# Mixed projection of a streaming encoder layer: where in the instruction stream the stationary operands of the next group are prepared

## The chip, the core and the metric

The kernel runs on one NeuronCore of a Trainium2 chip. The metric is the device time of one execution, in microseconds (us); a kernel's time is the median over its runs. Engines are called as in the profile: PE is TensorE (PEld its weight loads), DVE is VectorE, ACT is ScalarE, POOL is GpSimd, SP is SyncE. POOL and SP also issue DMAs, each in the order of its own queue.

## What is computed

One layer of a hybrid encoder for two groups of requests together: 256 new frames of one stream and 16 frames each of 8 running streams, 384 rows in all, model width 2048. The part that matters here is the second branch of the mixer and its gate:

```python
a_ssd = gated_rmsnorm(y.reshape(b, L, D_INNER), z, p['ssd_norm'])   # 384 rows x 4096
br_pool = a_pool @ p['w_pool_proj']
br_ssd = a_ssd @ p['w_ssd_proj']                                    # 4096 x 2048
merged = gates[:, :, 0] * br_pool + gates[:, :, 1] * br_ssd
out = merged @ p['w_out']
```

Everything is float32. Each product of two float32 matrices is made of three products of rounded parts: an operand is split into a high part (rounded copy, made by ACT) and a low part (the difference, made by DVE), and PE adds high x high, high x low and low x high.

## The kernel before, in words

The layer runs in stages: normed input projections, pooling branch, state-space branch, then the **mixed projection** (`a_ssd @ w_ssd` woven together with the gate projections), then `w_out` and the MLP. In all of them PE multiplies tiles of 128 partitions, and a weight tile of 128 x 1024 is brought in by SP, split by ACT (the `wh_` tile) and by DVE (the `wl_` tile), and used by PE.

In the mixed projection, the 4096 rows of `w_ssd` are cut into eight **groups** `gk` = 0 to 7, and a group's output columns into two **halves** of 1024 (`np_` = 0, 1). A 2 x 2 block product is done with seven multiplications instead of eight, so that a half consists of seven **forms**, in this order: `b11, b21, U, b22, W, V, X` (`ORDER`). A form is one weight tile: a block as loaded (`b11, b21, b22`) or a sum of blocks (`U, W, V, X`, built in place by POOL's adding DMA, L1136, and by DVE, L1159). So a group has fourteen forms, numbered here t = 0 to 13, and the stage has 112. A form multiplies its weight with one or two **slots**, stationary tiles that hold blocks of `a_ssd` or differences of them; there are ten slots to a group:

```python
USES = {"b11": ((0, 0), (7, 2)), "b21": ((1, 3), (7, 5)), "b22": ((2, 8), (8, 9)),
        "X": ((3, 4),), "U": ((4, 6),), "W": ((5, 7),), "V": ((6, 1), (8, 2))}   # form: (product, slot)
DIFFS = ((6, 1, 4), (7, 0, 6), (8, 3, 7), (9, 5, 2), (1, 1, 0))                 # slot o = slot a - slot b
KEYS = {"b11": (0,), "s2": (2,), "b21": (3, 5), "U": (6,), "b22": (8, 9), "W": (7,), "V": (1,), "X": (4,)}
```

For each group the slots are prepared in three steps while the group before is multiplied. `aload` (L1232) brings the six raw blocks into the tile `ax` with four DMAs on POOL's queue, at t = 4 of the group before. There is one `ax` tile, so these DMAs wait until the last reader of the old contents, the refill of `X` (DVE's `alX`), is done. `diffs` (L1241) makes the five differences with five subtractions of 128 x 256 on DVE. `refill` (L1248 and L1249) splits one or two slots: ACT writes the high part (`ahb`, `ahU`, `ahs` and so on), DVE the low part (`alb`, `alU`, `als`). The high and low tiles exist once for each key, twice for `s2`; a key is refilled after its last use in the old group and before its first in the new one.

`quad` gives for each form the steps `ready` (split the weight, L1123 on ACT and L1124 on DVE, and build the next sum on DVE, L1159) and `run` (its matmuls, L1172 to L1174, then the products that are complete are taken to `acs`, L1149 and L1151), and at the end of `run` calls `extra(t)`, which emits the step of preparation for that t. `later()` places such a step behind the weight splits that were emitted last on ACT and DVE.

Between the forms stand the gate projections `ga` and `gb` (L102 to L104, with splits at L71 and L72): after each half of a gate projection three or four forms follow. A finished gate is scaled on DVE (`gat`, L1330), put through a sigmoid on ACT and multiplied on DVE (L1334). Within these rules a scheduler sets the order of the instructions on each engine; each engine then works through its own list in that order.

Of the kernel before, what the change touches and what calls it, by code (L numbers as in the profile page):

```python
# [33 lines left out]
def build(ctx, tc, io):  # L34
# [18 lines left out]
    def sstile(name):  # L53
        return pss.tile([P, 512], F32, tag="ss", name=name)
# [23 lines left out]
    @contextmanager  # L78
    def later():
        with behind(cut[0]), behind(cut[1]):  # L80
            yield
# [294 lines left out]
    with tc.tile_pool(name="phc", bufs=1, reuse_waits="tile") as pc, tc.tile_pool(name="phc2", bufs=2, reuse_waits="tile") as pc2:  # L376
# [3 lines left out]
        for i in range(2):  # L380
            b = pc.tile([P, 640], F32, name=f"pbuf{i}")[:, :519]
# [210 lines left out]
    with tc.tile_pool(name="phd", bufs=2, reuse_waits="tile") as pd, tc.tile_pool(  # L592
# [5 lines left out]
        for i in range(3):  # L598
            b = pd1.tile([P, 24, 19], F32, name=f"cbuf{i}")
# [513 lines left out]
    DIFFS = ((6, 1, 4), (7, 0, 6), (8, 3, 7), (9, 5, 2), (1, 1, 0))  # L1113
# [121 lines left out]
        raw.append(x)  # L1235
        return i

    def diffs(gk):
        x = raw[gk]
        for o, a, b in DIFFS:  # L1240
            v.tensor_tensor(x[:, o], x[:, a], x[:, b], ALU.subtract)  # L1241

    def refill(gk, key):
        ss = KEYS[key]
        n = len(ss)
        src = raw[gk][:, ss[0] : ss[-1] + 1 : max(1, ss[-1] - ss[0])]
        h, l = (pqf.tile([P, n, 2, P], F32R, tag=f"a{a}{key}", name=f"a{a}{key}{gk}", bufs=2 if key == "s2" else 1) for a in "hl")
        s.activation(h, src, AF.Copy)  # L1248
        v.tensor_tensor(l, src, h.bitcast(F32), ALU.subtract)  # L1249
        for i, j in enumerate(ss):  # L1250
            slots[gk][j] = (h[:, i], l[:, i])

    def sp_quad(gk, np_):
        def part(slot, k2):
            h, l = slots[gk][slot]
            return h[:, k2], l[:, k2]

        def extra(i):
            t = np_ * 7 + i
            if gk and t < 3:  # L1260
                with later():
                    refill(gk, ("W", "V", "X")[t])
            if gk == 7:
                if t == 4:
                    early = pq.tile([P, 10, 2, P], F32, tag="ax", name="axe").rearrange("p s k t -> p (s k t)")
                    for n in range(3):
                        place[n] = early[:, n * 768 : n * 768 + 768]
                        fetch(n)
                elif t == 6:
                    todo.extend(converted(lambda m: acc[:, m]))  # L1270
                elif t > 6:
                    todo.pop(0)()
                return
            if t == 4:
                aload(gk + 1)
            with later():
                if t == 9:
                    diffs(gk + 1)
                elif t == 10:
                    refill(gk + 1, "b11")  # L1280
                    refill(gk + 1, "s2")
                elif t > 10:
                    refill(gk + 1, ("b21", "U", "b22")[t - 11])

        return quad(f"sq{gk}_{np_}", pqw, acc, np_, gk == 0, lambda i, nb: io["w_ssd"][nb, gk * 2 + i], part, extra)

    todo, place = [], {}

    def fetch(n):
        if n not in place:  # L1290
            place[n] = pqw.tile([P, 1024], F32, tag="wd", name=f"mw{n}", bufs=7)
        gp.dma_start(place[n][:, :T], gb_scr[n])
        gp.dma_start(place[n][:, T : 2 * T], ma_scr[n])
# [152 lines left out]
    with tc.tile_pool(name="phf", bufs=1, side="right", reuse_waits="tile") as pf, tc.tile_pool(  # L1446
# [80 lines left out]
        for nb in range(4):  # L1527
# [3 lines left out]
            o = [sstile(f"wo{nb}_{b}") for b in range(3)] if nb else o_first  # L1531
# [168 lines left out]
    with tc.tile_pool(name="phg", bufs=1, side="right", reuse_waits="tile") as pg, tc.tile_pool(  # L1700
# [83 lines left out]
        for nb in range(4):  # L1784
            o = [sstile(f"wd{c8}_{nb}_{b}") for b in range(3)]
# [161 lines left out]
```

## Time and profile before

| what | value |
|---|---|
| median of 3 runs | 2588.47 us (2587.6 to 2589.66) |
| profiled execution, its own time | 2588.24 us |
| its span (first to last instruction) | 2586.5 us |
| PE busy over the span | 2572.9 us (99%) |
| DVE, ACT, POOL busy over the span | 1951.8, 1599.2, 446.4 us |
| mixed projection, 1106 to 1452 us of the span | 346 us; PE busy 342.42, DVE 287.01, ACT 274.04 us |
| granted TensorE clock | 0.999 |

The profiled execution's own time is 1.7 us longer than its span. It lies 0.2 us under the median. Times in the rows are microseconds from the span's start. A row of the timeline has start, duration, engine, line, operation, and the tiles written and read, without their numbers; the brackets at its end say how long the engine stood before it, and what released it. The ends of matmuls are modelled: the profiler gives a 128 x 384 matmul 0.33 us though the next one starts 0.16 us after it. DVE and ACT rows may overlap in the same way, by about 0.1 us.

### The profile page before, as it was taken

How to read it: one execution, taken by the hardware profiler on the slowest of the kernel's cores; microseconds unless marked ns; L12 is line 12 of the kernel's file. 1: busy time of each engine (PE TensorE's matmuls, PEld its weight loads, DVE VectorE, ACT ScalarE, POOL GpSimd, SP SyncE). 2: the span in 40 equal slices, each digit the busy share in tenths (PEclk: the TensorE clock that was granted, in tenths of full speed). 3: DMA queues.
4: the chain of work that ended last, by engine and by line, in shares of the span. 5: the costliest groups of instructions: out<-in, count | busy, mean ns of one | idle time of the engine just before them, and what ended most of it. 6: DMA issues, size and time to landing. Idle time of an engine off the chain costs nothing.

```text
span 2586.5 us, 41046 instructions
## 1 busy us (share of the span) xinstructions
PE 2572.9 (99%) x15589; PEld 2448.1 (95%) x15589; DVE 1951.8 (75%) x2763; ACT 1599.2 (62%) x2520; POOL 446.4 (17%) x647
## 2 busy tenths in 40 slices
PE   9999999999999999999999999999999999999998
PEld 9999999999999999998888988999999999999997
DVE  6676367999999999678878855767777777777766
ACT  6443355657565665578878634666766667676653
POOL 0000043355444444111111200000000000000000
PEclk9999999999999999999999999999999999999999
DMA  7444566666766676676666555654555555455444
GB/s 280 150 134 160 166 224 211 226 217 229 240 223 223 222 242 223 213 247 186 205 200 188 179 205 193 205 161 148 156 161 165 168 157 153 150 161 163 139 139 171
DMA packets 141782, 490.43 MB, mean 190 GB/s; under 512 B 21728, under 2 KB 26144, under 8 KB 135824
## 3 DMA queue, kind: packets, MB, share of 16 engines
q1 hardware_dynamic: 100544, 355.93, 41.1%
q0 software_dynamic: 33984, 117.06, 15.7%
q10 hardware_dynamic: 7056, 14.81, 1.8%
q8 instruction: 122, 2.00, 0.3%
q14 instruction: 76, 0.62, 0.1%
HBM read 437.85 MB, written 49.87 MB: 189 GB/s over the span
## 4 chain that ended last, share of the span: by engine, by line
PE 96%; DVE 2%; ACT 1%; issue 1%; DMA 1%; DVEq 0%; POOL 0%; ACTq 0%; POOLq 0%
PE pj_up L102 6%; PE pj_up L104 6%; PE pj_up L103 6%; PE wd L1173 5%; PE wd L1174 5%; PE wd L1172 5%; PE pj_x L102 5%; PE pj_x L103 5%; PE pj_x L104 5%; PE pj_z L104 3%; PE pj_z L102 3%; PE pj_z L103 3%; PE sq L1173 2%; PE sq L1174 2%; PE sq L1172 2%; PE pj_pp L102 2%
## 5 line engine op out<-in xcount | busy, mean ns | idle before, releaser
L102 PE MATMUL pj_up<-x1h,wh_up 128*128 128x384 f32 (+1 forms) x1024 | 333.7, 326 | 0.0
L103 PE MATMUL pj_up<-x1l,wh_up 128*128 128x384 f32 (+1 forms) x1024 | 333.4, 326 | 0.0
L104 PE MATMUL pj_up<-x1h,wl_up 128*128 128x384 f32 (+1 forms) x1024 | 333.4, 326 | 0.0
L71 ACT ACTIVATE wh_up<-w_up 128x1024 fp32r<-128x1024 f32 x126 | 133.2, 1057 | 219.2 <-PE pj_up L103 206.1
L102 PE MATMUL pj_x<-xgh,wh_x 128*128 128x384 f32 x768 | 251.9, 328 | 0.0
L103 PE MATMUL pj_x<-xgl,wh_x 128*128 128x384 f32 x768 | 250.4, 326 | 0.0
L104 PE MATMUL pj_x<-xgh,wl_x 128*128 128x384 f32 x768 | 250.4, 326 | 0.0
L72 DVE TENSOR_TENSOR wl_up<-w_up,wh_up 128x1024 fp32r<-128x1024 f32 x126 | 154.1, 1223 | 56.3 <-ACT wh_up L71 56.2
L103 PEld LDWEIGHTS pj_up<-x1l,wh_up 128*128 128x128 f32 x1024 | 193.6, 189 | 2.6
L102 PEld LDWEIGHTS pj_up<-x1h,wh_up 128*128 128x128 f32 x1024 | 193.6, 189 | 2.6
L104 PEld LDWEIGHTS pj_up<-x1h,wl_up 128*128 128x128 f32 x1024 | 193.6, 189 | 0.0
L102 PE MATMUL pj_z<-xgh,wh_z 128*128 128x384 f32 x512 | 166.9, 326 | 0.0
L103 PE MATMUL pj_z<-xgl,wh_z 128*128 128x384 f32 x512 | 166.9, 326 | 0.0
L104 PE MATMUL pj_z<-xgh,wl_z 128*128 128x384 f32 x512 | 166.9, 326 | 0.0
L1136 POOL DMA_DIRECT2D w_b_wd<-w_down x28 | 24.2, 864 | 773.4 <-DMA w_b_wd<-w_down 682.9
L102 PEld LDWEIGHTS pj_x<-xgh,wh_x 128*128 128x128 f32 x768 | 145.1, 189 | 2.1 <-issue 0.4
L103 PEld LDWEIGHTS pj_x<-xgl,wh_x 128*128 128x128 f32 x768 | 145.2, 189 | 0.0
L104 PEld LDWEIGHTS pj_x<-xgh,wl_x 128*128 128x128 f32 x768 | 145.2, 189 | 0.0
L72 DVE TENSOR_TENSOR wl_x<-w_x,wh_x 128x1024 fp32r<-128x1024 f32 x96 | 116.7, 1220 | 29.2 <-ACT wh_x L71 29.2
L71 ACT ACTIVATE wh_x<-w_x 128x1024 fp32r<-128x1024 f32 x96 | 100.4, 1052 | 61.1 <-PE pj_z L103 30.5
L1149 ACT COPY acc<-wd 128x512 f32<-128x512 f32 x200 | 116.6, 583 | 22.8 <-PE wd L1174 22.7
L1172 PE MATMUL wd<-wh_b_wd,fh 128*128 128x512 f32 x336 | 127.3, 379 | 0.0
(478 smaller groups left out, 7832.3 us busy)
## 6 DMA issues: line engine op xcount, KB each, us to landing
w_up<-w_up SPq DMA_DIRECT2D x128, 512.0 KB, 4.0
w_b_wd<-w_down SPq DMA_DIRECT2D x112, 512.0 KB, 4.5
w_x<-w_in SPq DMA_DIRECT2D x96, 512.0 KB, 3.9
w_z<-w_in SPq DMA_DIRECT2D x64, 512.0 KB, 4.3
w_b_sq<-w_ssd SPq DMA_DIRECT2D x64, 512.0 KB, 4.7
w_ga<-w_ga SPq DMA_DIRECT2D x32, 512.0 KB, 4.6
w_pp<-w_pp SPq DMA_DIRECT2D x32, 512.0 KB, 3.5
hs<-ssm POOLq DMA_DIRECT2D x16, 1024.0 KB, 7.2
```

What stands on the lines that cost most here:

```text
L71: cut[0] = s.activation(h, w, AF.Copy)
L72: cut[1] = v.tensor_tensor(l, w, h.bitcast(F32), ALU.subtract)
L102: te.matmul(out, wh, xh, start=first, stop=False, **how)
L103: te.matmul(out, wh, xl, start=False, stop=False, **how)
L104: return te.matmul(out, wl, xh, start=False, stop=last, **how)
L1136: gp.dma_start(w, unit(0, np_ * 2), accum_op=ALU.add)
L1149: s.copy(dst, o)
L1172: te.matmul(out, mh, vh, start=begin, stop=False, skip_group_check=held)
L1173: te.matmul(out, mh, vl, start=False, stop=False, skip_group_check=held)
L1174: te.matmul(out, ml, vh, start=False, stop=end, skip_group_check=held)
```

## The change

The same operations are done on the same data; where they are emitted differs. Before, group gk + 1 was prepared in eight forms: t = 9 to 13 of group gk (`diffs`; `b11` and `s2`; `b21`; `U`; `b22`) and t = 0 to 2 of group gk + 1 (`W`, `V`, `X`). After, it is prepared in t = 6 to 13 and 0 to 3: `s2` at t = 6, three differences at t = 7 and two at t = 8, nothing at t = 9 and 10, `b11`, `b21`, `U` at t = 11, 12, 13, then `b22`, `W`, `V`, `X` at t = 0 to 3 of the new group. `diffs` takes a slice of the table for this. The load stays at t = 4. Lines behind the change have numbers smaller by one in the changed kernel (L1330 becomes L1329).

```diff
-    def diffs(gk):
+    def diffs(gk, which=slice(0, 5)):
         x = raw[gk]
-        for o, a, b in DIFFS:
+        for o, a, b in DIFFS[which]:
             v.tensor_tensor(x[:, o], x[:, a], x[:, b], ALU.subtract)
...
-            if gk and t < 3:
+            if gk and t < 4:
                 with later():
-                    refill(gk, ("W", "V", "X")[t])
+                    refill(gk, ("b22", "W", "V", "X")[t])
...
             with later():
-                if t == 9:
-                    diffs(gk + 1)
-                elif t == 10:
-                    refill(gk + 1, "b11")
+                if t == 6:
                     refill(gk + 1, "s2")
+                elif t in (7, 8):
+                    diffs(gk + 1, slice(0, 3) if t == 7 else slice(3, 5))
                 elif t > 10:
-                    refill(gk + 1, ("b21", "U", "b22")[t - 11])
+                    refill(gk + 1, ("b11", "b21", "U")[t - 11])
```

The pieces of the engines' lists below are from group 4. The names carry the group: `ax5` is the raw tile of group 5, `wl_W_sq4_1` the low weight part of form W in half 1 of group 4, `alb115` the low stationary part for `b11` of group 5; `alX4` belongs to group 4.

**Second half of group 4.** DVE before, from behind the split of `U` and the first of the five differences, to the gate's split:

```order
L1151 TENSOR_TENSOR acs_12341<-sq4_1_7_14424,acs_12341 128x512
L1159 TENSOR_TENSOR w_b12_sq4_1_14432<-w_b12_sq4_1_14432,w_b22_sq4_1_14439 128x1024
L1241 TENSOR_TENSOR ax5_14355<-ax5_14355 128x256 x4
L1124 TENSOR_TENSOR wl_b22_sq4_1_14531<-w_b22_sq4_1_14439,wh_b22_sq4_1_14530 128x1024
L1159 TENSOR_TENSOR w_b11_sq4_1_14435<-w_b12_sq4_1_14432,w_b11_sq4_1_14435 128x1024
L1249 TENSOR_TENSOR alb115_14551<-ax5_14355,ahb115_14550 128x256
L1249 TENSOR_TENSOR als25_14555<-ax5_14355,ahs25_14554 128x256
L1124 TENSOR_TENSOR wl_W_sq4_1_14559<-w_b12_sq4_1_14432,wh_W_sq4_1_14558 128x1024
L1159 TENSOR_TENSOR w_b21_sq4_1_14437<-w_b21_sq4_1_14437,w_b12_sq4_1_14432 128x1024
L1249 TENSOR_TENSOR alb215_14573<-ax5_14355,ahb215_14572 128x512
L1330 TENSOR_TENSOR gat12_14576<-pj_ga12_14363,rstd_197 128x384
L72 TENSOR_TENSOR wl_ga13_0_14583<-w_ga13_0_14580,wh_ga13_0_14582 128x1024
```

DVE after, from the same split of `U` on:

```order
L1159 TENSOR_TENSOR w_b12_sq4_1_14436<-w_b12_sq4_1_14436,w_b22_sq4_1_14443 128x1024
L1151 TENSOR_TENSOR acs_12341<-sq4_1_7_14424,acs_12341 128x512
L1124 TENSOR_TENSOR wl_b22_sq4_1_14535<-w_b22_sq4_1_14443,wh_b22_sq4_1_14534 128x1024
L1159 TENSOR_TENSOR w_b11_sq4_1_14439<-w_b12_sq4_1_14436,w_b11_sq4_1_14439 128x1024
L1159 TENSOR_TENSOR w_b21_sq4_1_14441<-w_b21_sq4_1_14441,w_b12_sq4_1_14436 128x1024
L1124 TENSOR_TENSOR wl_W_sq4_1_14555<-w_b12_sq4_1_14436,wh_W_sq4_1_14554 128x1024
L1249 TENSOR_TENSOR alb115_14569<-ax5_14355,ahb115_14568 128x256
L1329 TENSOR_TENSOR gat12_14572<-pj_ga12_14363,rstd_197 128x384
L72 TENSOR_TENSOR wl_ga13_0_14579<-w_ga13_0_14576,wh_ga13_0_14578 128x1024
L1333 TENSOR_TENSOR gat12_14572<-gat12_14572,ppt12_14396 128x384
L1124 TENSOR_TENSOR wl_V_sq4_1_14611<-w_b11_sq4_1_14439,wh_V_sq4_1_14610 128x1024
L1249 TENSOR_TENSOR alb215_14631<-ax5_14355,ahb215_14630 128x512
```

Four of the differences shown (the fifth stands one row ahead), `als25` and `alb215` no longer stand between the split of `U` and the split `wl_ga13_0`; `alb215` stands behind the split of `V`.

PE before, at the place where that gate projection begins:

```order
L1174 MATMUL sq4_1_5_14535<-wh_W_sq4_1_14558,alW4_14245 128x512
L102 MATMUL pj_ga13_14579<-xgh0_263,wh_ga13_0_14582 128x384
L103 MATMUL pj_ga13_14579<-xgl0_264,wh_ga13_0_14582 128x384
L1172 MATMUL sq4_1_6_14563<-wh_V_sq4_1_14614,ahV4_14298 128x512
L1172 MATMUL sq4_1_8_14517<-wh_V_sq4_1_14614,ahs24_14114 128x512
L104 MATMUL pj_ga13_14579<-xgh0_263,wl_ga13_0_14583 128x384
```

PE after, the same place:

```order
L1174 MATMUL sq4_1_5_14539<-wh_W_sq4_1_14554,alW4_14295 128x512
L102 MATMUL pj_ga13_14575<-xgh0_263,wh_ga13_0_14578 128x384
L103 MATMUL pj_ga13_14575<-xgl0_264,wh_ga13_0_14578 128x384
L104 MATMUL pj_ga13_14575<-xgh0_263,wl_ga13_0_14579 128x384
L102 MATMUL pj_ga13_14575<-xgh1_284,wh_ga13_0_14578 128x384
L103 MATMUL pj_ga13_14575<-xgl1_285,wh_ga13_0_14578 128x384
```

The two matmuls of form V that stood ahead of the first one with `wl_ga13_0` are gone from there; form V now follows the whole half projection.

**First half of group 4, the last reader of `ax4`.** DVE before, from the split of `U`:

```order
L1124 TENSOR_TENSOR wl_U_sq4_0_14303<-w_b12_sq4_0_14216,wh_U_sq4_0_14302 128x1024
L1249 TENSOR_TENSOR alX4_14318<-ax4_13953,ahX4_14317 128x256
L1159 TENSOR_TENSOR w_b12_sq4_0_14216<-w_b12_sq4_0_14216,w_b22_sq4_0_14223 128x1024
L1159 TENSOR_TENSOR w_b11_sq4_0_14219<-w_b12_sq4_0_14216,w_b11_sq4_0_14219 128x1024
L1159 TENSOR_TENSOR w_b21_sq4_0_14221<-w_b21_sq4_0_14221,w_b12_sq4_0_14216 128x1024
L1124 TENSOR_TENSOR wl_b22_sq4_0_14322<-w_b22_sq4_0_14223,wh_b22_sq4_0_14321 128x1024
L1151 TENSOR_TENSOR acs_12341<-sq4_0_7_14204,acs_12341 128x512
L1124 TENSOR_TENSOR wl_W_sq4_0_14342<-w_b12_sq4_0_14216,wh_W_sq4_0_14341 128x1024
```

DVE after, from the split of `U`:

```order
L1124 TENSOR_TENSOR wl_U_sq4_0_14299<-w_b12_sq4_0_14212,wh_U_sq4_0_14298 128x1024
L1249 TENSOR_TENSOR alV4_14314<-ax4_13953,ahV4_14313 128x256
L1159 TENSOR_TENSOR w_b12_sq4_0_14212<-w_b12_sq4_0_14212,w_b22_sq4_0_14219 128x1024
L1159 TENSOR_TENSOR w_b11_sq4_0_14215<-w_b12_sq4_0_14212,w_b11_sq4_0_14215 128x1024
L1159 TENSOR_TENSOR w_b21_sq4_0_14217<-w_b21_sq4_0_14217,w_b12_sq4_0_14212 128x1024
L1124 TENSOR_TENSOR wl_b22_sq4_0_14318<-w_b22_sq4_0_14219,wh_b22_sq4_0_14317 128x1024
L1151 TENSOR_TENSOR acs_12341<-sq4_0_7_14200,acs_12341 128x512
L1249 TENSOR_TENSOR alX4_14338<-ax4_13953,ahX4_14337 128x256
```

`alX4`, on which the four DMAs into `ax5` wait, stood right behind the split of `U` and now stands behind three sums, the split of `b22` and an addition to `acs`.

**End of the first half of group 4, the first reader of `ax5`.** ACT before, from the split of form X:

```order
L1123 ACTIVATE wh_X_sq4_0_14418<-w_b21_sq4_0_14221 128x1024
L1144 COPY sq4_1_0_14422<-acs_12341 128x512
L1144 COPY sq4_1_1_14445<-acs_12341 128x512
L1123 ACTIVATE wh_b11_sq4_1_14441<-w_b11_sq4_1_14435 128x1024
L1149 COPY acs_12341<-sq4_0_6_14346 128x512
L1123 ACTIVATE wh_b21_sq4_1_14460<-w_b21_sq4_1_14437 128x1024
```

ACT after:

```order
L1123 ACTIVATE wh_X_sq4_0_14418<-w_b21_sq4_0_14217 128x1024
L1144 COPY sq4_1_0_14422<-acs_12341 128x512
L1248 ACTIVATE ahs25_14432<-ax5_14355 128x256
L1144 COPY sq4_1_1_14449<-acs_12341 128x512
L1123 ACTIVATE wh_b11_sq4_1_14445<-w_b11_sq4_1_14439 128x1024
L1149 COPY acs_12341<-sq4_0_6_14346 128x512
L1123 ACTIVATE wh_b21_sq4_1_14467<-w_b21_sq4_1_14441 128x1024
```

`ahs25`, which reads what the four DMAs brought, now stands one copy behind the split of X, ahead of the splits of the second half's `b11` and `b21`.

## The prediction

> **What bounds the kernel now.** I read the chain that ended last, then the waits of PE, then PE's timeline in the mixed projection. The chain's shares by engine:
>
> ```profile
> PE 96%; DVE 2%; ACT 1%; issue 1%; DMA 1%; DVEq 0%; POOL 0%; ACTq 0%; POOLq 0%
> ```
>
> PE sets the end, and whatever PE loses between two matmuls is lost to the kernel; work on DVE or ACT costs nothing by itself. So the question is what PE still loses and whether the change touches it. PE's waits over the whole program, without those of the first microseconds (columns: who, for whom, total us, times, longest):
>
> ```profile
> PE pj_ga L104 <- DVE wl_ga L72: 2.4, 3, 1.0
> ...
> PE pj_ga L102 <- ACT wh_ga L71: 0.3, 1, 0.3
> PE sq L1173 <- DVE wl_V_sq L1124: 0.3, 2, 0.2
> PE pj_gb L102 <- ACT wh_gb L71: 0.3, 1, 0.3
> ```
>
> All of it lies in the mixed projection, 3.3 us together. But the ends of matmuls are modelled, and a wait shorter than the modelled tail doesn't appear. Starts are better. Undisturbed, a 128 x 384 matmul starts 0.16 us after the one before it and a 128 x 512 one needs 0.215. Here are starts in the second half of group 4:
>
> ```profile
> 1317.87 0.33 PE L103 MATMUL pj_ga<-xgl,wh_ga 128*128 128x384 f32 x1
> 1318.15 0.48 PE L1172 MATMUL sq<-wh_V_sq,ahV 128*128 128x512 f32 x1
> 1318.47 0.38 PE L1172 MATMUL sq<-wh_V_sq,ahs 128*128 128x512 f32 x1
> 1319.86 0.43 PE L104 MATMUL pj_ga<-xgh,wl_ga 128*128 128x384 f32 x1 [1.01 <-DVE wl_ga L72]
> 1320.12 0.33 PE L102 MATMUL pj_ga<-xgh,wh_ga 128*128 128x384 f32 x1
> ```
>
> From 1317.87 to 1318.15 there are 0.28 us instead of 0.16, then 0.32, 1.39 and 0.26 instead of 0.215, 0.215 and 0.16: 0.12 + 0.10 + 1.17 + 0.10 = 1.49 us lost, where the bracket shows 1.01. I took the starts of all matmuls of the stage in this manner. Losses above 0.05 us stand at one place in each group, always in the second half, while the next group is prepared: 0.10 in group 0, then 0.85, 0.36, 1.49, 1.49, 1.02 and 0.97 in groups 1 to 6, together 6.28 us. Group 7 prepares nothing and has 0.23 in its first half. Groups 1 and 6 begin like this:
>
> ```profile
> 1181.76 0.38 PE L1172 MATMUL sq<-wh_W_sq,ahW 128*128 128x512 f32 x1
> 1182.73 0.43 PE L104 MATMUL pj_ga<-xgh,wl_ga 128*128 128x384 f32 x1 [0.59 <-DVE wl_ga L72]
> ...
> 1408.63 0.38 PE L1172 MATMUL sq<-wh_V_sq,ahs 128*128 128x512 f32 x1
> 1409.29 0.43 PE L102 MATMUL pj_gb<-xgh,wh_gb 128*128 128x384 f32 x1 [0.28 <-ACT wh_gb L71]
> ...
> 1410.04 0.48 PE L1173 MATMUL sq<-wl_V_sq,ahV 128*128 128x512 f32 x1 [0.16 <-DVE wl_V_sq L1124]
> ```
>
> A second view of the same thing is PE's weight loads, whose ends are not stretched (same columns):
>
> ```profile
> PEld pj_ga L104 <- DVE wl_ga L72: 4.0, 4, 1.4
> PEld sq L1173 <- DVE wl_V_sq L1124: 0.9, 2, 0.5
> PEld pj_ga L102 <- ACT wh_ga L71: 0.7, 1, 0.7
> PEld pj_gb L102 <- ACT wh_gb L71: 0.7, 1, 0.7
> PEld sq L1172 <- ACT wh_V_sq L1123: 0.7, 2, 0.4
> PEld pj_gb L104 <- DVE wl_gb L72: 0.3, 1, 0.3
> ```
>
> That is 7.3 us, with group 7's 0.3 in it; it counts the shortened lead of the loads too, so I keep 6.28. [...]
>
> **The change part by part.** First what is taken from in front of the late split. DVE in the second half of group 4:
>
> ```profile
> 1307.75 1.23 DVE L1124 TENSOR_TENSOR wl_U_sq<-w_b_sq,wh_U_sq 128x1024 fp32r<-128x1024 f32 x1 [1.25 <-ACT wh_U_sq L1123]
> 1308.89 0.42 DVE L1241 TENSOR_TENSOR ax<-ax 128x256 f32<-128x256 f32 x1
> ...
> 1310.96 1.42 DVE L1241 TENSOR_TENSOR ax<-ax 128x256 f32<-128x256 f32 x4
> ...
> 1314.91 0.42 DVE L1249 TENSOR_TENSOR als<-ax,ahs 128x256 fp32r<-128x256 f32 x1
> ...
> 1317.52 0.69 DVE L1249 TENSOR_TENSOR alb<-ax,ahb 128x512 fp32r<-128x512 f32 x1
> ...
> 1318.59 1.22 DVE L72 TENSOR_TENSOR wl_ga<-w_ga,wh_ga 128x1024 fp32r<-128x1024 f32 x1
> ```
>
> From the split of U at 1307.75 DVE never stands, and the gate's low part is ready at 1318.59 + 1.22 = 1319.81; PE wanted it one step after 1317.87, at 1318.03. The changed order has the same rows between the split of U and this one, less the five differences (0.34 + 1.34 of DVE's time by the distances of starts), `als` (0.33) and the two-slot `alb` (0.60): 2.61 us. The split starts at 1315.98 and ends at 1317.20, 0.8 us ahead of its use. The split of U, where the backlog begins, waits for ACT (1.25 us in its bracket), so it stays where it is. Half the form V that the program's order had put ahead of the gate's low products goes back behind them, so V's split too has a half projection more.
>
> The same 2.6 us is freed in each of the other groups, whose loss is 1.49 at most. In groups 5 and 6 the late ones are ACT's high part of the gate and V's low part; there form V now comes whole ahead of the gate, so that the gate's high part is needed 2.2 us later (ten matmuls of 0.215), and V's low part has the 1.7 us of the differences and the 0.3 of `als` less in front of it, against 0.33 lost. All of 6.28 us can go.
>
> What is moved has to fit elsewhere. `als` and the differences go to t = 6 to 8, ahead of the split of U that waits 1.25 us for ACT, and the splits before it wait as well: these 2.0 us go into idle time of DVE and cost nothing. `ahs` goes with it on ACT, 0.31 us in front of a split that waits for PE. The two-slot refill `b22` goes to t = 0, so that three refills stand ahead of U's split in the first half where two did and `alX` does after it. DVE in the first half of group 4:
>
> ```profile
> 1285.44 1.23 DVE L1124 TENSOR_TENSOR wl_U_sq<-w_b_sq,wh_U_sq 128x1024 fp32r<-128x1024 f32 x1 [0.53 <-ACT wh_U_sq L1123]
> 1286.58 0.42 DVE L1249 TENSOR_TENSOR alX<-ax,ahX 128x256 fp32r<-128x256 f32 x1
> 1286.92 3.61 DVE L1159 TENSOR_TENSOR w_b_sq<-w_b_sq,w_b_sq 128x1024 f32<-128x1024 f32 x3
> 1290.45 1.22 DVE L1124 TENSOR_TENSOR wl_b_sq<-w_b_sq,wh_b_sq 128x1024 fp32r<-128x1024 f32 x1
> 1291.59 0.68 DVE L1151 TENSOR_TENSOR acs<-sq,acs 128x512 f32<-128x512 f32 x1
> ```
>
> PE's first use of the split at 1290.45:
>
> ```profile
> 1291.99 0.38 PE L1173 MATMUL sq<-wl_b_sq,ahb 128*128 128x512 f32 x1
> ```
>
> The 0.60 us of the longer `alb` falls before U's split and its 0.53 us wait, and `alV` (0.34) takes the place behind U that `alX` had, so the split of `b22` keeps its 1290.45 and is ready at 1291.67, 0.32 us ahead of its use at 1291.99. That is the thinnest cover in the change. If it is gone the price is between nothing and 0.60 - 0.32 = 0.28 us for each of groups 1 to 6, 1.7 us in all; since a wait of DVE lies in between I take 0.1 a group, 0.6 us. `alX`, behind the additions, delays the gate's split there by 0.34; I take that as covered, with 0.3 us for the whole stage as its upper end.
>
> Then the queue that is moved past: POOL. Its four loads into `ax` wait for `alX`:
>
> ```profile
> 1287.30 0.76 POOL L1232 DMA_DIRECT2D ax<-a_scr  x1 [9.22 <-DVE alX L1249]
> ```
>
> Behind them in POOL's queue are the store of a gate product, which waits for DVE in any case, the fetch of a pooling product and the adding DMA of a later quad. `alX` moves from 1286.58 behind three sums, a split and an addition, to 1291.59 + 0.60 = 1292.19, 5.6 us later. The four loads, at 0.76 each, then start from 1292.9 to 1295.2. The time from issue to landing of all loads into `ax`, least, median and most:
>
> ```profile
> DMA to landing us min/median/max: 2.8/3.1/7.0
> ```
>
> The last lands at 1298.3 by the median. Its first reader is now `ahs` on ACT, behind the split of X and one copy:
>
> ```profile
> 1296.82 1.07 ACT L1123 ACTIVATE wh_X_sq<-w_b_sq 128x1024 fp32r<-128x1024 f32 x1
> 1297.78 1.12 ACT L1144 COPY sq<-acs 128x512 f32<-128x512 f32 x2
> 1299.60 1.06 ACT L1123 ACTIVATE wh_b_sq<-w_b_sq 128x1024 fp32r<-128x1024 f32 x1 [0.70 <-PE pj_ga L103]
> ```
>
> That is 1297.78 + 0.52 = 1298.3: the load arrives just in time, where before it landed 5.6 us sooner and was first read by the difference at 1308.89. Behind `ahs` stand the splits of the second half's `b11` and `b21`, and the split of `b11` itself waits 0.70 us for PE. Its low part on DVE, and PE's first use of that:
>
> ```profile
> 1300.69 1.23 DVE L1124 TENSOR_TENSOR wl_b_sq<-w_b_sq,wh_b_sq 128x1024 fp32r<-128x1024 f32 x1 [1.53 <-ACT wh_b_sq L1123]
> ```
>
> ```profile
> 1303.66 0.38 PE L1173 MATMUL sq<-wl_b_sq,ahb 128*128 128x512 f32 x1
> ```
>
> It is ready at 1300.69 + 1.23 = 1301.92 and used 1.74 us later. With 0.70 - 0.31 of ACT's wait, `ahs` may be 2.1 us late before PE stands, a landing of 5.2 us. I set this at nothing, with the range's upper end from the row's 7.0.
>
> The sum against the profiled execution: 2588.24 - 6.28 + 0.6 = 2582.6 us. The median lies 0.23 above it, so 2582.8 us. Nothing behind the stage takes this back, since the chain has PE in 96% of the span and no other wait for data; the work behind it starts as much earlier.
>
> **The rivals.** (1) *Half the cover.* The backlog is only partly removed: the thin 0.3 us ahead of `b22` breaks in the first halves (1.7 us), and where V and the gate changed places 1 to 2 us of the old loss remains. For it: group 4's split would be just 0.8 us early, and DVE is as busy over a group as before. Against it: DVE's and ACT's waits for PE and each other in between. The gain is 2 to 5 us: 2585.2 us, with 2583.5 to 2586.5 around it.
>
> (2) *No gain.* The modelled tails mislead in the other way, or the losses move from the gate's split to the next tight one, the first half's `b22`. Then less than 2 us is left: 2587.5 us. Against it: 1.39 us between two starts cannot be a tail.
>
> (3) *Slower: the load of `ax` lands late.* It decides from 5.2 us of landing time on. The row's most is 7.0. If the loads take that, PE stands 7.0 - 5.2 = 1.8 us in each of six groups, 10.8 us, and as ACT then comes late into the second half, I let half of the old loss come back: 2588.5 - 3.1 + 10.8 = 2596.2 us. For it: a load that was read 15 us after it landed is now read as it lands. Against it: the row's median of 3.1.
> [...]
>
> That the change doesn't do what it says is excluded by the order of instructions.
>
> **How the numbers follow.** A measurement of this kernel can tell about 0.2%, 5.2 us, from no change. My forecast, most of the 6.28 us gone, has 0.60; (1) has 0.22; (2) 0.10; (3) 0.08. The forecast's own range is 2581.5 (all of it gone, and 0.7 below for the 7.3 of the weight loads) to 2584.2 (with the 1.7 of the thin cover). A fifth or so of it lies above 2583.3, the limit of 0.2%, hence 0.48 for faster from it and 0.04 from the lower edge of (1): 0.52. Within 0.2%: 0.12 + 0.18 + 0.10 = 0.40. Slower: 0.08. For 8 in 10 the range is 2581.2 to 2587.0: it holds the forecast and (1) and leaves out most of (2) and (3).
>
> **What would show it.** Right: in the second halves PE's starts run through at 0.16 and 0.215 us, with the waits for `wl_ga`, `wl_V`, `wh_ga` and `wh_gb` gone; only group 7's 0.23 stays. DVE's bracket ahead of U's split in the second half shrinks. `ahs` follows its copy without a bracket that names the DMA. Wrong: brackets at `b22` in first halves, or at `ahs` with PE standing at the `b11` or gate that follows; or the starts run through and the time stays.

## The result, and the profile after

| | median us | runs | ratio to before (95% interval) |
|---|---|---|---|
| before | 2588.39 (2587.6 to 2589.66) | 10 | |
| changed | 2581.7 (2580.95 to 2582.6) | 10 | 0.9974 (0.9964 to 0.9984) |
| changed, repeated beside three of the experiments (before there: 2588.36) | 2581.58 (2580.99 to 2582.24) | 8 | 0.9974 (0.9964 to 0.9984) |

The change saves 6.7 us, 0.26%. The profiled execution, the slowest of the ten, took 2582.6 us, 5.64 less than that of before: the mixed projection became 6.18 us shorter (below) and began 0.55 later.

The chain that ended last, by engine, and all the waits of PE in the whole program, in the profile of the changed kernel:

```profile
PE 99%; ACT 0%; DVE 0%; DMA 0%; DVEq 0%; issue 0%
```

```profile
PE warm_o L250 <- DVE warm L246: 1.2, 1, 1.2
PE pj_p L326 <- ACT xgh L286: 0.2, 1, 0.2
```

PE had 96% of the chain before and has 99% now. Both waits that are left lie in the first microseconds; all those of the mixed projection are gone. (Between starts the 0.23 us of group 7 stayed, as forecast.) PE's timeline where the late split of group 4 is used:

```profile
1315.37 0.38 PE L1174 MATMUL sq<-wh_W_sq,alW 128*128 128x512 f32 x1
1315.58 0.33 PE L102 MATMUL pj_ga<-xgh,wh_ga 128*128 128x384 f32 x1
1315.74 0.33 PE L103 MATMUL pj_ga<-xgl,wh_ga 128*128 128x384 f32 x1
1315.91 0.33 PE L104 MATMUL pj_ga<-xgh,wl_ga 128*128 128x384 f32 x1
1316.07 0.33 PE L102 MATMUL pj_ga<-xgh,wh_ga 128*128 128x384 f32 x1
```

The starts run through at 0.21 and 0.16 us, and the gate comes whole, without two matmuls of `V` in it. DVE's timeline in front of it:

```profile
1305.69 1.22 DVE L1124 TENSOR_TENSOR wl_U_sq<-w_b_sq,wh_U_sq 128x1024 fp32r<-128x1024 f32 x1
...
1313.23 0.41 DVE L1249 TENSOR_TENSOR alb<-ax,ahb 128x256 fp32r<-128x256 f32 x1
1313.56 0.55 DVE L1329 TENSOR_TENSOR gat<-pj_ga,rstd 128x384 f32<-128x384 f32 x1
1314.03 1.21 DVE L72 TENSOR_TENSOR wl_ga<-w_ga,wh_ga 128x1024 fp32r<-128x1024 f32 x1
...
1315.89 1.23 DVE L1124 TENSOR_TENSOR wl_V_sq<-w_b_sq,wh_V_sq 128x1024 fp32r<-128x1024 f32 x1 [0.18 <-ACT wh_V_sq L1123]
```

The gate's low part is ready at 1314.03 + 1.21 = 1315.24, 0.67 us ahead of its use at 1315.91, where it had been 1.8 us late. DVE even has to wait again, 0.18 us at the split of `V`.

From the first matmul of the mixed projection's products (`sq`) to the last start there were 351.27 us (1106.11 to 1457.38) and are 345.09 (1106.66 to 1451.75): 6.18 us less. Here is PE's loss between starts, by group, for the two kernels and for four of the experiments below (second halves of groups 0 to 6; us; read as in the prediction, each row from one profiled execution):

| kernel | 0 | 1 | 2 | 3 | 4 | 5 | 6 | sum | length of the stage against before |
|---|---|---|---|---|---|---|---|---|---|
| before | 0.10 | 0.85 | 0.36 | 1.49 | 1.49 | 1.02 | 0.97 | 6.28 | |
| changed | 0 | 0 | 0 | 0 | 0.15 | 0 | 0 | 0.15 | -6.18 |
| differences only | 0 | 0 | 0.06 | 0.51 | 0.38 | 0 | 0 | 0.95 | -5.39 |
| s2 only | 0.10 | 0.52 | 0 | 1.15 | 1.14 | 1.01 | 0.95 | 4.87 | -1.41 |
| b22 only | 0.11 | 0.51 | 0 | 0.90 | 0.90 | 1.11 | 0.91 | 4.44 | -1.89 |
| changed, six more differences | 0 | 0.76 | 1.18 | 1.13 | 1.01 | 1.36 | 1.03 | 6.47 | +0.17 |

The sums and the lengths of the stage, which are read independently, agree within 0.1 us in every row.

Two things moved that nobody waited for before. In the first half of group 4 the two-slot `alb` stands far ahead, with waits of DVE behind it, the split of `b22` kept its place behind the sums, and `alX` went behind it:

```profile
1277.56 0.68 DVE L1249 TENSOR_TENSOR alb<-ax,ahb 128x512 fp32r<-128x512 f32 x1
...
1283.21 1.23 DVE L1124 TENSOR_TENSOR wl_U_sq<-w_b_sq,wh_U_sq 128x1024 fp32r<-128x1024 f32 x1 [0.53 <-ACT wh_U_sq L1123]
...
1288.22 1.22 DVE L1124 TENSOR_TENSOR wl_b_sq<-w_b_sq,wh_b_sq 128x1024 fp32r<-128x1024 f32 x1
1289.36 0.68 DVE L1151 TENSOR_TENSOR acs<-sq,acs 128x512 f32<-128x512 f32 x1
1289.96 0.41 DVE L1249 TENSOR_TENSOR alX<-ax,ahX 128x256 fp32r<-128x256 f32 x1
```

```profile
1289.71 0.38 PE L1173 MATMUL sq<-wl_b_sq,ahb 128*128 128x512 f32 x1
```

The low part of `b22` is ready at 1289.44 and used at 1289.71: the thin cover is 0.27 us, and it held. The loads into `ax` start 5.6 us later in the group, as forecast, but they also land later; their time from issue to landing over the program, then ACT and DVE at the start of the second half of group 4:

```profile
DMA to landing us min/median/max: 2.8/5.0/7.5
```

```profile
1297.54 0.42 ACT L1248 ACTIVATE ahs<-ax 128x256 fp32r<-128x256 f32 x1 [1.44 <-DMA ax<-a_scr]
```

```profile
1301.02 0.88 DVE L1241 TENSOR_TENSOR ax<-ax 128x256 f32<-128x256 f32 x2 [0.34 <-DMA ax<-a_scr]
```

The median was 3.1 us before. In group 4 `ahs` waited 1.44 us for the first pair of loads and the differences 0.34 for the second, and PE lost 0.15 us, the only loss left in the table.

### The profile page after: what moved, and what is told of

Its sections match the earlier page's. It is cut to its first block, busy times and chain, and to the rows that moved or that the text cites. A ratio compares the mean times of both kernels' runs of the same rounds, so it can differ in the third digit from the quotient of the medians.

```text
span 2580.8 us, 41038 instructions
## 1 busy us (share of the span) xinstructions
PE 2570.9 (100%) x15589; PEld 2449.3 (95%) x15589; DVE 1953.0 (76%) x2763; ACT 1597.7 (62%) x2520; POOL 446.1 (17%) x647
## 4 chain that ended last, share of the span: by engine, by line
PE 99%; ACT 0%; DVE 0%; DMA 0%; DVEq 0%; issue 0%
PE pj_up L102 6%; PE pj_up L103 6%; PE pj_up L104 6%; PE wd L1174 5%; PE wd L1173 5%; PE wd L1172 5%; PE pj_x L102 5%; PE pj_x L104 5%; PE pj_x L103 5%; PE pj_z L104 3%; PE pj_z L103 3%; PE pj_z L102 3%; PE sq L1173 3%; PE sq L1174 3%; PE sq L1172 3%; PE pj_gb L102 2%
```

## The experiments

**Theory.** PE lost time because DVE (and ACT) had a backlog in front of the split that comes late in each second half; the change takes work out of that backlog. Rivals: that only the new order of PE matters (the gate whole, instead of with `V` in it), that one part does everything, and, for the risk, that the late loads into `ax` are what can make it slower. Differences between kernels are a few us of 2588, so where the interval of a ratio touches 1, the verdict rests on the losses between PE's starts.

**One part alone: the differences** (kernel before, with this edit; `diffs` takes a slice as in the changed kernel; PE's order becomes that of the changed kernel):

```diff
-                if t == 9:
-                    diffs(gk + 1)
+                if t in (7, 8):
+                    diffs(gk + 1, slice(0, 3) if t == 7 else slice(3, 5))
```

> The kernel before with one part of the change: the five differences go from t = 9 to t = 7 and 8; s2, b11, b21, U and b22 stay. Theory (backlog): DVE's queue ahead of the late split in each second half is 1.68 us shorter, which covers the largest loss of a group (1.49), so nearly all of 6.28 us goes: 2582 to 2583 us, 5.5 to 6.3 below before, PE's starts running through in the second halves, and no later landing of the loads into ax than before (median near 3.1 us), since alX stays where it was. Rival (each part is needed, the gain adds up in proportion to the time freed, 1.68 of 2.61): about 4 us, 2584.4. Rival (the gain comes from moving b22, or from the earlier copy of s2 on ACT): less than 1.5 us, 2587 or more.

Measured: 2583.39 us (11 runs), ratio 0.9981 (0.9972 to 0.999), 4.9 us below before; landing 3.2 us median. So most, not all: PE's timeline in group 4 still has a gap.

```profile
1316.25 0.33 PE L103 MATMUL pj_ga<-xgl,wh_ga 128*128 128x384 f32 x1
1316.68 0.43 PE L104 MATMUL pj_ga<-xgh,wl_ga 128*128 128x384 f32 x1
1316.95 0.33 PE L102 MATMUL pj_ga<-xgh,wh_ga 128*128 128x384 f32 x1
```

Between 1316.25 and 1316.68 are 0.43 us in place of 0.16. The expectation compared 1.68 us freed with a loss of 1.49. But the low part had been 1.78 us late (1319.81 against 1318.03 in the prediction's rows): two matmuls of `V` had filled part of the wait, and with the gate whole that filling is gone. A matmul started 0.05 us after its split was ready (1319.86 against 1319.81), so 1.78 + 0.05 - 1.68 = 0.15 of lateness remain by that count; 0.38 was measured. DVE's rows show where the rest comes from:

```profile
1306.13 1.23 DVE L1124 TENSOR_TENSOR wl_U_sq<-w_b_sq,wh_U_sq 128x1024 fp32r<-128x1024 f32 x1 [1.17 <-ACT wh_U_sq L1123]
1307.39 1.22 DVE L1159 TENSOR_TENSOR w_b_sq<-w_b_sq,w_b_sq 128x1024 f32<-128x1024 f32 x1
...
1315.41 1.22 DVE L72 TENSOR_TENSOR wl_ga<-w_ga,wh_ga 128x1024 fp32r<-128x1024 f32 x1
```

Behind U's split DVE starts its next row after 1.26 us, where it was 1.14 in the prediction's rows: 0.12 more, so that PE stood 0.27 (the split is ready at 1316.63, wanted at 1316.41). The start behind the stand came 0.11 late as well (0.27 us for 0.16), about as behind the stands in the prediction's rows (0.10): 0.38 together.

**One part alone: `s2`.**

```diff
-                if t == 9:
+                if t == 6:
+                    refill(gk + 1, "s2")
+                elif t == 9:
                     diffs(gk + 1)
                 elif t == 10:
                     refill(gk + 1, "b11")
-                    refill(gk + 1, "s2")
```

> The kernel before with s2 alone moved, from t = 10 to t = 6. Theory (backlog): 0.33 us of DVE and 0.31 of ACT are freed in front of the late split, so each of the groups 1 to 4 gives back 0.33, and in groups 5 and 6, where PE's order becomes that of the changed kernel (V whole ahead of the gate), most of the 1.0 goes: 1.3 to 3.3 us, 2585.1 to 2587.1, with wl_ga still waited for in groups 1, 3 and 4 (0.5, 1.2 and 1.2 us between starts). Rival (order: what matters is that PE no longer takes two matmuls of the gate and then V): groups 5 and 6 alone, 2.0 us, groups 1 to 4 unchanged.

Measured: 2586.78 us (11 runs), ratio 0.9995 (0.9986 to 1.0004). By the table groups 1 to 4 gave back 0.33, 0.36, 0.34 and 0.35, one `als` (0.33) each, as the backlog says. Groups 5 and 6 gave back nothing, though PE's order there is that of the changed kernel but for one matmul with `ahs`. That refutes the rival of order alone, and my own expectation for these two groups as well. PE and DVE in group 5:

```profile
1361.86 0.38 PE L1172 MATMUL sq<-wh_V_sq,ahV 128*128 128x512 f32 x1
1362.07 0.38 PE L1172 MATMUL sq<-wh_V_sq,ahs 128*128 128x512 f32 x1
1363.20 0.48 PE L1173 MATMUL sq<-wl_V_sq,ahV 128*128 128x512 f32 x1 [0.75 <-DVE wl_V_sq L1124]
```

```profile
1361.93 1.22 DVE L1124 TENSOR_TENSOR wl_V_sq<-w_b_sq,wh_V_sq 128x1024 fp32r<-128x1024 f32 x1
```

With `V` whole ahead of the gate its low part is wanted right behind two matmuls, at 1362.29; before, two matmuls of the gate and the 0.59 us that PE stood for them lay in between. So the new order wants it 0.9 us earlier, and 0.33 us freed doesn't pay for that (0.43 + 0.91 - 0.33 = 1.01, which is the loss measured).

**One part alone: `b22` and the shift of the refills.**

```diff
-            if gk and t < 3:
+            if gk and t < 4:
                 with later():
-                    refill(gk, ("W", "V", "X")[t])
+                    refill(gk, ("b22", "W", "V", "X")[t])
...
                 elif t == 10:
-                    refill(gk + 1, "b11")
                     refill(gk + 1, "s2")
                 elif t > 10:
-                    refill(gk + 1, ("b21", "U", "b22")[t - 11])
+                    refill(gk + 1, ("b11", "b21", "U")[t - 11])
```

> The kernel before with the refills alone shifted by one form: b11, b21 and U at t = 11 to 13, b22 at t = 0 of the next group, W, V and X at t = 1 to 3; differences and s2 stay at t = 9 and 10. Theory (backlog): 0.60 us of DVE are freed ahead of the late split, so groups 1, 3 and 4 give back 0.6 each and group 2 its 0.36, and groups 5 and 6, whose order becomes that of the changed kernel, most of 1.0 each: 3 to 4.2 us, 2584.2 to 2585.4. The thin cover of the first half's b22 holds as in the changed kernel. alX moves with this part, so the loads into ax land later (median near 5 us) but are read only by s2 and the differences much later, so nothing waits for them. Rival (order alone): 2.0 us from groups 5 and 6.

Measured: 2586.35 us (11 runs), ratio 0.9993 (0.9984 to 1.0002); landing 4.9 us median, with nothing waiting for it. Groups 3 and 4 gave back 0.59 each, group 2 its 0.36, group 1 only 0.34. Group 6 gave back 0.06 and group 5 lost 0.09 more, for the reason just shown: PE's order in these two groups is now wholly that of the changed kernel, with the low part of `V` wanted behind one matmul instead of two, another 0.2 us earlier. The expected 3 to 4.2 us were too much mainly by those two groups.

The three parts alone shorten the stage by 5.39 + 1.41 + 1.89 = 8.7 us, together by 6.18: they draw on the same lost time, and once it is gone a further part brings only cover.

**More backlog: four differences twice** (kernel before; `diffs` takes a slice here too):

```diff
                 if t == 9:
+                    diffs(gk + 1, slice(0, 4))
                     diffs(gk + 1)
```

> The kernel before with four of the five differences of the next group done twice at t = 9 (the second time with the same result): 1.34 us more of DVE ahead of the late split in each of seven groups. Theory (backlog): groups 1 to 6, which have no cover left, lose 1.34 us more each, group 0 up to 1.3: 8.0 to 9.4 us, 2596.4 to 2597.8, less what the changed order of PE takes back by putting whole runs ahead of the gate (down to 5 us, 2593.5). Rival (DVE's backlog is not what is late; PE's starts are set by ACT's high parts or the order): under 2 us, 2590.5 or less.

Measured: 2596.59 us (5 runs), ratio 1.0032 (1.002 to 1.0045), 8.3 us slower. 1.34 us more of DVE in seven groups is 9.4 us, so nearly all of it came out at PE. The backlog is the cause, and it had no cover.

**Back into the changed kernel: six differences more.**

```diff
+                elif t == 10:
+                    diffs(gk + 1, slice(1, 4))
+                    diffs(gk + 1, slice(1, 4))
                 elif t > 10:
```

> The changed kernel with three of the differences done twice over again at t = 10 (with the same result): 2.0 us more of DVE ahead of the late split in each second half, where the change had taken 2.61 away. Theory A (cover as the trace of after shows it: 1.2, 1.2, 0.8, 0.55, 0.6, 0.25 and 0.3 us ahead of the gate's low products in groups 0 to 6): PE loses what goes over, 0.8, 0.8, 1.2, 1.45, 1.4, 1.75 and 1.7, about 9 us, less 0.4 in groups 3 and 4, where PE's order puts two matmuls of V back in between: 2588 to 2591, as slow as before or slower, though 0.6 us less lies in the way. Theory B (the arithmetic of the prediction run backwards: each group loses its old loss less 0.6): 3 us, 2584 to 2586. The two differ by whether PE's changed order has itself used up cover.

Measured: 2588.57 us (11 runs), ratio 1.0001 (0.9992 to 1.001). 2.0 us a group given back undo the whole gain, where 2.61 had been taken away. That speaks for theory A: 0.76, 1.18, 1.13 and 1.01 us in groups 1 to 4 against 0.8, 1.2, 1.05 and 1.0 expected (the last two with `V` in between), though groups 0, 5 and 6 lost 0.8, 0.4 and 0.7 less than it gives. So the cover in front of the late split, as 2.0 us less the loss (and less 0.4 for the two matmuls of `V` in groups 3 and 4), was 0.5 to 1.2 us in groups 1 to 4, 0.6 and 1.0 in groups 5 and 6 and at least 2.0 in group 0. In groups 1 to 6 that is less than the freed time less the old loss, which is 1.1 to 2.3 there.

**The loads one form later** (changed kernel; rival 3 of the prediction made to happen):

```diff
-            if gk and t < 4:
+            if gk and t in (0, 1, 2, 4):
                 with later():
-                    refill(gk, ("b22", "W", "V", "X")[t])
+                    refill(gk, ("b22", "W", "V", "", "X")[t])
```

> The changed kernel with the refill X, and so the loads into ax behind it, at t = 4 in place of 3; PE's order of matmuls is unchanged. In the changed kernel alX let the loads of group 4 go at 1290.67, ahs waited 1.44 us for them and PE lost 0.15; in the other groups ahs just didn't wait. One form is about 3 us. Theory (rival 3 of the prediction is real and was just missed: ACT has about 1.3 us to spare ahead of the second half's first splits): ahs waits 3 us in five groups and 4.5 in group 4, and PE stands for what is over 1.3 us, 1.7 and 3 us: 6 to 13 us slower than the changed kernel, 2588 to 2595. Rival (ACT's idle time covers it, the load doesn't matter): under 2 us slower. [...]

Measured: 2599.7 us (5 runs), ratio 1.0042 (1.003 to 1.0055), 18.1 us slower than the changed kernel. `ahs` waited in all six groups; ACT in group 1, and PE's timeline behind it:

```profile
1168.87 0.42 ACT L1248 ACTIVATE ahs<-ax 128x256 fp32r<-128x256 f32 x1 [4.66 <-DMA ax<-a_scr]
```

```profile
1168.08 0.38 PE L1174 MATMUL sq<-wh_X_sq,alX 128*128 128x512 f32 x1
1170.76 0.43 PE L102 MATMUL pj_ga<-xgh,wh_ga 128*128 128x384 f32 x1 [2.31 <-ACT wh_ga L71]
...
1172.03 0.43 PE L104 MATMUL pj_ga<-xgh,wl_ga 128*128 128x384 f32 x1 [0.67 <-DVE wl_ga L72]
...
1172.97 0.53 PE L103 MATMUL pj_ga<-xgl,wh_ga 128*128 128x384 f32 x1
1173.29 0.53 PE L104 MATMUL pj_ga<-xgh,wl_ga 128*128 128x384 f32 x1
```

The waits of `ahs` in groups 1 to 6 (4.66, 5.09, 3.61, 2.89, 2.04, 1.66 us) cost PE 3.51, 3.94, 2.55, 1.18, 0.33 and 0 us of standing, 11.5 together. So `ahs` may wait 1.1 to 1.7 us before PE notices, and from there on each microsecond counts. The stage became 17.7 us longer than the changed kernel's; the other 6 us are a price that nobody had set: after the long stands of groups 1 to 3 the matmuls start 0.32 us apart instead of 0.16, as in the last two rows. The granted clock stands in the column behind POOL's, in stretches of 4 us:

```profile
1168.00:1172.00 4.00, 1.05 (x5) 0.35 (x3) 1.68 (x3) 3.13 (x5) 0.00 (x0) 1.00 1.01 291
1172.00:1176.00 4.00, 3.98 (x15) 3.98 (x16) 3.97 (x7) 1.58 (x3) 0.00 (x0) 0.61 0.70 189
1176.00:1180.00 4.00, 4.00 (x22) 3.68 (x21) 2.09 (x4) 2.54 (x4) 0.00 (x0) 0.96 0.02 6
```

The run shows the landing under another load of DVE as well. The loads into `ax` landed after 5.8 us by the median; in groups 1 to 3 it was 5.7, 6.6 and 6.1 us, with DVE busy for only 3.0 to 3.5 of 7 us around them and a DMA share of 0.91 to 0.92. In the changed kernel it was 4.3, 4.4 and 5.1 us in these groups, with DVE busy for 6.03, 6.03 and 5.19 of 7.5 us and a DMA share of 0.81 to 0.87. Under a DVE with less to do they came later, not sooner, so DVE's operations are not what holds them up.

**`s2` behind the differences** (changed kernel):

```diff
-                if t == 6:
+                if t == 9:
                     refill(gk + 1, "s2")
```

> The changed kernel with the refill s2 at t = 9, behind the differences, in place of t = 6; PE's order is unchanged. Theory: ahs no longer waits for the loads in group 4 (1.44 us there), nor can it where they land late, and als still goes ahead of the late split's backlog or costs 0.33 us of 0.3 to 0.7 that were to spare in groups 3 to 6: the time of the changed kernel within 0.05%, 2581 to 2583, with the 0.15 us of group 4 gone. Rival (als at t = 9 stands in front of the late split again and ends its cover): up to 0.2 us in groups 5 and 6 and nothing elsewhere, still under 2583.5. If it is more, the cover ahead of the late split was smaller than the trace of after shows.

Measured: 2582.31 us (11 runs), ratio 0.9976 (0.9967 to 0.9984), the changed kernel within the interval. `ahs` waits for no load any more, yet PE still lost 0.22 us at the same place in group 4, so that loss isn't from `ahs`. DVE there:

```profile
1300.92 0.89 DVE L1241 TENSOR_TENSOR ax<-ax 128x256 f32<-128x256 f32 x2 [1.45 <-DMA ax<-a_scr]
...
1302.66 1.22 DVE L1124 TENSOR_TENSOR wl_b_sq<-w_b_sq,wh_b_sq 128x1024 fp32r<-128x1024 f32 x1
```

The differences wait for the second pair of loads, and the split behind them is late. **The changed kernel again**, without an edit, run beside it:

> The changed kernel as it is, run beside the three others so that they can be compared on one chip: 2581 to 2583 us, and again a wait of ahs for the loads in one or two groups at most, with PE losing under 0.3 us to it. If the landing of the loads differs from execution to execution, another group than 4 can show it.

Measured: 2581.58 us (8 runs). It has the opposite pair: `ahs` waits 1.54 us in group 4, the differences don't wait, and PE loses nothing there. So the 0.15 us of the first trace doesn't stand in every execution.

**The differences one form later** (changed kernel):

```diff
-                elif t in (7, 8):
-                    diffs(gk + 1, slice(0, 3) if t == 7 else slice(3, 5))
+                elif t in (8, 9):
+                    diffs(gk + 1, slice(0, 3) if t == 8 else slice(3, 5))
```

> The changed kernel with the five differences at t = 8 and 9 in place of 7 and 8. Theory: the 0.15 to 0.22 us that PE loses at the start of group 4's second half comes from the differences, which wait on DVE for the second pair of loads (1.45 us with s2 out of the way) and hold up a split behind them, not from ahs; one form later they find their data, and that loss is gone. In exchange two differences (0.67 us) come to stand behind the split of U, ahead of the late split: where the changed kernel has 0.25 to 0.6 us to spare there (groups 3 to 6), PE loses 0.1 to 0.45 each, 1 us in all. So 2582 to 2583.5, no better than the changed kernel. Rival (ahs's wait makes that loss): it stays at 1304.

Measured: 2582.17 us (9 runs), ratio 0.9976 (0.9966 to 0.9986). The loss at the start of the second half isn't there; but it wasn't in the repeated run of the changed kernel either, so this trace alone says nothing of its cause. New ones stand in the first half of group 4 (0.16) and in groups 5 and 6 (0.10 and 0.11), less than expected. No gain.

**Why the loads land late.** Two kernels. The first takes a weight buffer away (changed kernel; the same number at the two other uses of the tiles `wd`):

```diff
-                w = pool.tile([P, 1024], F32, tag="wd", name=f"w_b{i}{j}_{nm}", bufs=7)
+                w = pool.tile([P, 1024], F32, tag="wd", name=f"w_b{i}{j}_{nm}", bufs=6)
```

> The changed kernel with six buffers in place of seven for the weight blocks of the mixed projection; PE's, ACT's and DVE's order in the stage is the same, SP's is not: the third load of each quad's four waits for a buffer and goes behind the gate's loads, and so some of SP's traffic no longer falls on the loads into ax. Theory (sharing): in windows of 7.5 us from alX on, DMA share falls below the 0.8 to 0.87 of the changed kernel, and the landing of the loads into ax with it, from 4.9 us median towards the 3.0 that they had at a share of 0.5 to 0.65; ahs of group 4 then waits less or not at all. If landing is set by anything else (the queue's own start, POOL's issue, DVE's accesses), it stays at 5 us though the share falls. The time: 2581 to 2585 us, slower than the changed kernel only if PE waits for late weights.

Measured: 2582.29 us (9 runs), ratio 0.9976 (0.9967 to 0.9986); landing 5.3 us median. But DMA's share stayed at 0.80 to 0.86 in the six windows, so the edit didn't do what it was for, and tells nothing of the cause. The second adds traffic instead (kernel before; `spare` is a scratch tensor in DRAM):

```diff
+            if t == 2:
+                with later():
+                    for k in range(2):
+                        s.dma_start(spare[gk * 2 + k], io["w_ssd"][k, gk * 2])
             if t == 4:
                 aload(gk + 1)
```

> The kernel before with traffic added where its loads into ax fly: ACT's queue starts two copies of 512 KB from DRAM to DRAM behind the refill X of each group (they serve nothing else). The loads start when they did, DVE's and PE's orders are those of before. Theory (sharing of the DMA engines sets the landing): in windows of 7.5 us from alX on, DMA share rises from 0.52 to 0.65 to 0.75 or more, and the landing of the loads into ax from 3.0 us towards the 4 to 6 of the changed kernel, so that the median over all is over 4. If the landing is set by DVE's work or by POOL, it stays at 3.1. Nothing waits for these loads in the order of before, so the time stays within 0.1% unless the adding loads of weights behind them come late too.

The 7.5 us behind `alX` in group 4, first of before, then changed, then with more traffic; each row has the span of time, its length, the busy time of PE, PEld, DVE, ACT and POOL, the clock, DMA's share and GB/s, and below it stands the landing of the loads into `ax` that were issued in it:

```profile
1286.60:1294.10 7.50, 7.50 (x38) 6.75 (x38) 7.47 (x10) 4.89 (x8) 3.00 (x4) 1.00 0.52 164
...
DMA to landing us min/median/max: 2.9/3.0/3.1
```

```profile
1290.00:1297.50 7.50, 7.50 (x43) 7.04 (x42) 6.02 (x8) 6.10 (x10) 4.11 (x6) 1.00 0.82 255
...
DMA to landing us min/median/max: 5.5/6.1/7.5
```

```profile
1290.30:1297.80 7.50, 7.50 (x38) 6.75 (x38) 7.47 (x10) 5.25 (x8) 3.00 (x4) 1.00 0.84 264
...
DMA to landing us min/median/max: 4.0/4.4/4.6
```

With the copies DVE is as busy as before (7.47 of 7.5 us) and POOL issues the same loads, but DMA's share goes from 0.52 to 0.84 and the landing from 3.0 to 4.4 us (over the program from 3.1 to 4.8). So other traffic on the DMA engines is enough to make these loads late. In the changed kernel that traffic is there: the loads now fly with SP's loads of the next half's weights, which were issued from 1289.47 on. The one run took 2593.36 us, beside 2588.61 for before, outside the 0.1% that I expected: PE lost 0.6 to 1.2 us more in first halves, at the gate's low part in group 0 and at the split of a block in groups 1, 2, 5 and 6. The scheduler had put ACT's split of the block behind one more copy there, so this time measures more than the traffic, and I didn't follow it further.

## Why the prediction was right

2582.8 us was forecast and 2581.7 measured. Step by step:

- *PE's loss read from starts (6.28 us), not from the shown waits (3.3).* Right: the stage became 6.18 us shorter, more than the shown waits could have given. (The second view there isn't free of overlap, as it was taken to be: PE's weight loads have 0.19 us each and start 0.16 apart. The sum doesn't use its 7.3 us, only the lower end of the range.)
- *Term A: 2.61 us freed on DVE cover every group's loss; the gate's low part of group 4 is then 0.8 us ahead.* Right, with 0.67 us; DVE stood 0.12 behind U's split here too (1305.69 to 1306.94, 1.25 us for 1.14). The working was looser than its result. For groups 5 and 6 it set the freed time against 0.33 us lost, where `V`'s new place in PE's order takes 1.1 us of it first (the 0.9 above, and 0.2 for one matmul less in front); with 2.0 us freed there that didn't matter, with 0.33 or 0.60 (the parts alone) it took all or nearly all of the gain.
- *Term B: 0.6 us for the thin cover in front of the first half's `b22`.* This term was too high: no first half lost anything, since the waits of DVE between the longer `alb` and the sums behind `U` (0.53 us in the row above) took it up. Without it the forecast would have been 2582.2. The cover is as thin as read (0.27 us), and in the run with more traffic such covers gave way.
- *Term C: the loads land 3.1 us after issue, just in time, and cost nothing.* The cost was 0.15 us, but the landing was mis-sized: 5.0 us by the median and 6.1 in group 4. The row of 3.1 was measured where the DMA share was 0.52 to 0.65, and the change moved the loads to where it is 0.79 to 0.87. That row held the sign itself: its longest landing, 7.0, belongs to the loads issued from 1102.47 on, just ahead of the stage, which landed after 6.0 to 7.0 us under a DMA share of 1.03. Two slips in the working went against each other: the second load is issued 0.54 us later than four issues of 0.76 in a row would have it, so the last would have landed at 1298.8; but `ahs` waits for the first pair alone (it ran at 1297.54, while the differences waited for the second pair until 1301.02). The sign that `ahs` would follow its copy without a bracket failed in group 4. That the cost stayed this small is in part luck: `ahs` waited 1.44 and 1.54 us in the two runs of the changed kernel, and ACT had 1.1 to 1.7 us to spare (the prediction's working gave 2.1).
- *Rivals 1 and 2, half the gain or none:* excluded by the table, where 0.15 us is left of 6.28.
- *Rival 3, slower by late loads:* its mechanism is real and was nearer than its chance of 0.08 said. `ahs` did wait in group 4, and with the loads one form later the kernel takes 1.0042 times (1.003 to 1.0055) the time of before. Its price left out the clock (0.56 to 0.61 in stretches of 4 us behind the long stands). DVE's work isn't what made the loads late: they landed in 3.0 us under a DVE that was busy for 7.47 of 7.5 us, and in 6.1 under one busy for 6.02.

No kernel tried beats the changed one beyond the intervals. What it could still gain in the stage is 0.23 us in group 7 and 0.15 in group 4.

## What to carry to other kernels

Where one engine sets the end, measure its loss by the distances of starts, and ask of each late operand by how much it is late; the loss is smaller if the order has other work to fill the wait (1.49 us lost for a split 1.78 us late), and that filler can vanish when the order changes. Steps that prepare the next round can be taken out of the busy stretch for nothing if they fit into an idle one, but look what their moving releases: here a load that starts 5.6 us later met a DMA share of 0.79 to 0.87 instead of 0.52 to 0.65 and landed after 5.0 us instead of 3.1 by the median, so the landing time has to be taken from a stretch that is as busy as the new place. Gains of parts that draw on one lost stretch don't add up (8.7 us alone, 6.18 together).

## What the runs showed of the hardware

The landing time of the same 192 KB loads, by medians of windows of 7 to 8 us, went from about 3 us (2.9 to 3.5) at a DMA share of 0.52 to 0.65 to 3.5 to 6.6 us at 0.75 to 0.92. The other traffic came from SP's queue in the changed kernel (3.5 to 6.1 us at 0.79 to 0.87) and from ACT's as well in the run with the copies (4.0 to 5.7 us at 0.77 to 0.88).

In the kernel with the later loads the matmuls ran at half pace behind the long stands of groups 1 to 3; in group 1 they start 0.32 us apart instead of 0.16 from 1172.97 to 1176.17. The granted clock, in stretches of 4 us, was 0.61 and 0.96 from 1172 to 1180, 0.59 and 0.56 from 1220 to 1228 and 0.59 from 1272 to 1276; in the 4 us before these it was 1.00, 1.00 and 0.99, and 1.00 behind the second and the third. With a clock of one half, as the doubled distance of starts has it, and 1 around it, these numbers give half pace for about 3.4, 6.8 and 3.4 us; that is an estimate. In the 4 us before each, PE was busy for 1.05, 1.74 and 1.97 us. The longest stand of group 1, by the distances of starts, was 2.5 us (1168.08 to 1170.76, less 0.215). In the kernel with the doubled differences a stand of 1.36 us in group 4 (1322.61 to 1324.19, less 0.215) did not bring this about: the starts from 1324.55 on are 0.26 and 0.16 us apart, and the clock of that run's span is 0.999, where it is 0.996 with the later loads. How long a stand it takes, no run here shows. The half pace made stands of 11.5 us cost 17.7.
